# A small store ahead of all others on the store ring, and final waits in the order of the stores, in a group softmax that streams 570 MB

## Chip, cores, metric

One core of one Trainium2 chip, the other cores idle. The time is device microseconds of one execution; lower is better.

## The reference

```python
def reference(x):                       # x: (4, 4096, 4352) float32
    B, N, D = x.shape
    G = 8
    x_g = x.reshape(B, N, G, D // G)
    x_g = x_g - x_g.max(axis=-1, keepdims=True)
    exp = np.exp(x_g)
    out = exp / exp.sum(axis=-1, keepdims=True)
    return out.reshape(B, N, D).astype(np.float32)
```

Softmax over groups of 544 values. The input is read once and the output written once: 285.2 MB each way.

## The kernel before

64 tiles of 256 rows; a tile is 128 partitions x 34816 bytes (4.46 MB), in one of six buffers. SyncE issues all loads (one DMA ring), ScalarE all stores (the other ring). VectorE takes the maxima and scales; ScalarE does the exponentials and their sums. Semaphores tie them together.

```python
    def take(engine, sem, n=1):
        engine.sem_inc(sem, -n).wait_op(sem, n, "sem-ge")
    # ... (vector_max, vector_scale, scalar_exp: one row of each tile half at a time)

    def store(b, target):
        take(nc.scalar, scaled, R)
        nc.scalar.dma_start(out=target, in_=bufs[b][:, :]).then_inc(stored[b], 16)

    def scalar_tile(j, *targets):
        take(nc.scalar, seen)
        for r in range(R):
            if r < len(targets):
                store((j - LAG + r) % NT, targets[r])
            scalar_exp(j * R + r)

    for t in range(nt):                                   # SyncE: loads
        b = t % NT
        if t >= NT:
            nc.sync.wait_ge(stored[b], 16 * (t // NT))
        nc.sync.dma_start(out=bufs[b][:, :], in_=xt[t]).then_inc(landed[b], 16)
    for b in range(NT):                                   # SyncE: the final waits
        nc.sync.wait_ge(stored[b], 16 * ((nt - b + NT - 1) // NT))

    nc.scalar.preload_act_table(Exp)                      # ScalarE
    for j in range(LAG):                                  # LAG = 2
        scalar_tile(j)
    with loop(nc.scalar) as u:
        for b in range(NT):
            scalar_tile(LAG + b, turn_out[u, b])          # first store: in here
    # ... (two last tiles, last stores; VectorE's program)
```

Of the kernel before, what the change touches and what calls it, by code (L numbers as in the profile page):

```python
# [1 line left out]

# [5 lines left out]


@with_exitstack  # L10
def kernel(
    ctx: ExitStack,
    tc: tile.TileContext,
    x: bass.AP,
    out: bass.AP,
):
    nc = tc.nc
    G = 8
    P = 128
    R = 2  # L20
    NT = 6
    S = R * NT
    LAG = 2
    xf = x.flatten_outer_dims()
    of = out.flatten_outer_dims()
    N, D = xf.shape
    Dg = D // G
    nt = N // (P * R)
    turns = (nt - LAG) // NT
    rest = LAG + turns * NT  # L30
    assert rest == nt - 2
    f32 = mybir.dt.float32
    X = mybir.AxisListType.X
    Exp = mybir.ActivationFunctionType.Exp
    xt = xf.rearrange("(t p r) d -> t p (r d)", p=P, r=R)
    ot = of.rearrange("(t p r) d -> t p (r d)", p=P, r=R)
    turn_out = of[:turns * S * P, :].rearrange("(u b p r) d -> u b p (r d)", b=NT, p=P, r=R)

    landed = [tc.alloc_semaphore(f"landed{b}") for b in range(NT)]
    stored = [tc.alloc_semaphore(f"stored{b}") for b in range(NT)]  # L40
    seen = tc.alloc_semaphore("seen")
    max_done = tc.alloc_semaphore("max_done")
    exp_done = tc.alloc_semaphore("exp_done")
    rec_done = tc.alloc_semaphore("rec_done")
    scaled = tc.alloc_semaphore("scaled")

    ctx.enter_context(tc.tile_critical(no_gpsimd_drain=True))  # L47
    bufs = [ctx.enter_context(nc.sbuf_tensor(f"xt{b}", [P, R * D], f32)) for b in range(NT)]
    mx = ctx.enter_context(nc.sbuf_tensor("mx", [P, S, G], f32))
    sm = ctx.enter_context(nc.sbuf_tensor("sm", [P, S, G], f32))  # L50
    rs = ctx.enter_context(nc.sbuf_tensor("rs", [P, S, G], f32))

    def loop(engine):

        return nc.Fori(
            0, turns, engines=OrderedEngineSet([engine.engine]), head_slot={engine.engine: 0})

    def take(engine, sem, n=1):
        engine.sem_inc(sem, -n).wait_op(sem, n, "sem-ge")  # L59

    def row(s):
        b, r = divmod(s, R)
        return bufs[b][:, r * D:(r + 1) * D].rearrange("p (g d) -> p g d", g=G)

    def vector_max(n):
        s = n % S
        if s % R == 0:
            take(nc.vector, landed[s // R], 16)
            nc.vector.sem_inc(seen, 1)
        nc.vector.reduce_max(out=mx[:, s, :], in_=row(s), axis=X, negate=True).then_inc(max_done, 1)  # L70

    def vector_scale(n):
        s = n % S
        take(nc.vector, exp_done)
        nc.vector.reciprocal(out=rs[:, s, :], in_=sm[:, s, :]).then_inc(rec_done, 1)  # L75
        take(nc.vector, rec_done)
        xr = row(s)
        for g in range(G):
            i = nc.vector.tensor_scalar_mul(  # L79
                out=xr[:, g, :], in0=xr[:, g, :], scalar1=rs[:, s, g:g + 1])  # L80
        i.then_inc(scaled, 1)

    def scalar_exp(n):
        s = n % S
        take(nc.scalar, max_done)
        xr = row(s)
        for g in range(G):
            i = nc.scalar.activation(  # L88
                out=xr[:, g, :],
                in_=xr[:, g, :],  # L90
                func=Exp,
                bias=mx[:, s, g:g + 1],
                scale=1.0,
                accum_out=sm[:, s, g:g + 1],
            )
        i.then_inc(exp_done, 1)
# [14 lines that stand above are left out]
    for t in range(nt):  # L111
        b = t % NT
        if t >= NT:
            nc.sync.wait_ge(stored[b], 16 * (t // NT))
        nc.sync.dma_start(out=bufs[b][:, :], in_=xt[t]).then_inc(landed[b], 16)
    for b in range(NT):
        nc.sync.wait_ge(stored[b], 16 * ((nt - b + NT - 1) // NT))


    nc.scalar.preload_act_table(Exp)  # L120
    for j in range(LAG):
        scalar_tile(j)
    with loop(nc.scalar) as u:
        for b in range(NT):
            scalar_tile(LAG + b, turn_out[u, b])
    scalar_tile(nt - 2, ot[nt - 4])
    scalar_tile(nt - 1, ot[nt - 3], ot[nt - 2])
    store((nt - 1) % NT, ot[nt - 1])


    def vector_rows(lo, hi):
        for n in range(lo, hi):
            vector_max(n + 1)
            vector_scale(n)

    vector_max(0)
    vector_rows(0, LAG * R)
    with loop(nc.vector):
        vector_rows(LAG * R, LAG * R + S)
    vector_rows(rest * R, nt * R - 1)  # L140
    vector_scale(nt * R - 1)


# [1 line left out]
_INS = ['x']  # L145
_OUTS = [((4, 4096, 4352), 'float32')]


# [23 lines left out]
```

## Time and profile before

| | before |
|---|---|
| time, median of 3 | 1330.06 us (1329.78 to 1330.08) |
| VectorE, ScalarE busy | 78%, 58% of the span |
| 16 DMA engines busy | 90% or more in 39 of 40 slices |
| first store's issue on ScalarE | 5.47 us; all others 0.34 to 0.35 |
| last store's landing on the 16 engines: middle, last | 1320.41, 1326.77 us |

Read the table from the bottom of the machine upwards: the DMA engines are full, so what changes the time is either bytes, or time in which an engine moves none, or the lag of the last engine. The lines themselves are in the prediction.

I use one derived quantity. **Lost time** at moment T is T minus the time that the bytes finished by then would have taken: T - (bytes finished by T) / (16 x 34816) x 1.2888 us. 1.2888 us is an eighth of the 10.31 us between landings of consecutive loads while only loads run, 8 packets per engine each. The bytes come from the trace's packet records, a packet in flight counted by its elapsed share. In the kernel before it is 2.81 us at 45 us (the start: the first packets begin at 1.96 us and last about 2.1 us) and 3.72 us at 66 us: 0.91 us is lost when the first store begins. After that it stays level or falls slowly.

### The profile page before, as it was taken

The page shows a single profiled execution, that of the slowest core. Times are in us where ns is not written, and L with a number is a line of the kernel's source. Part 1 is how long each engine was busy: PE and PEld are TensorE (multiplying, and loading weights), DVE is VectorE, ACT ScalarE, POOL GpSimd, SP SyncE. Part 2 cuts the span into 40 slices and gives each one's busy share as a digit, 9 for nine tenths or more (in the row PEclk, how much of TensorE's full clock was granted, in tenths as well). Part 3 has the DMA queues.
Part 4 walks back from the last instruction along what each step waited for, and adds up shares of the span by engine and source line. Part 5 has one row for each costly group of instructions (what it writes and reads, how often), then busy time and mean ns, then how long its engine had stood idle before and what let it go on. Part 6 is the DMA issues. An engine that isn't in the chain of part 4 may idle for free. (4 is left out here: it accounts for less than half of the span.)

```text
span 1328.5 us, 4328 instructions
## 1 busy us (share of the span) xinstructions
DVE 1041.7 (78%) x1280; ACT 764.5 (58%) x2049; POOL 0.2 (0%) x4
## 2 busy tenths in 40 slices
DVE  5899987887877878778787787877878778787781
ACT  3677755655556556565565655655556555565551
POOL 0000000000000000000000000000000000000000
DMA  9999999999999999999999999999999999999997
GB/s 403 418 436 435 434 433 429 432 435 436 435 433 428 432 435 436 435 434 430 429 436 435 435 434 433 426 436 436 434 434 433 427 435 436 435 434 433 427 433 328
DMA packets 18439, 570.49 MB, mean 429 GB/s; under 512 B 2048, under 2 KB 2048, under 8 KB 2048
## 3 DMA queue, kind: packets, MB, share of 16 engines
q1 hardware_dynamic: 9216, 285.22, 49.8%
q10 hardware_dynamic: 9216, 285.22, 49.7%
q14 instruction: 7, 0.06, 0.0%
HBM read 285.21 MB, written 285.21 MB: 429 GB/s over the span
## 5 line engine op out<-in xcount | busy, mean ns | idle before, releaser
L88 ACT ACTIVATE xt<-xt,mx 128x544 f32<-128x544 f32 x1024 | 751.3, 735 | 534.1 <-ACTq L59 534.1
L70 DVE TENSOR_REDUCE mx<-xt 128x8 f32<-128x4352 f32 x128 | 599.2, 4682 | 238.3 <-DVEq L59 235.3
L79 DVE TENSOR_SCALAR xt<-xt,rs 128x544 f32<-128x544 f32 x1024 | 434.2, 498 | 19.2
L88 ACT ACTIVATION_READ_ACCUMULATOR xt<-xt,mx 128x1 f32 x1024 | 192.0, 187 | 0.0
L75 DVE RECIPROCAL rs<-sm 128x8 f32<-128x8 f32 x128 | 24.8, 193 | 4.2 <-DVEq L59 4.2
L120 ACT ACT_TABLE_LOAD x1 | 1.3, 1283 | 0.9 <-SPq L47 0.9
L156 POOL MEMSET const-bfloat16-1.0<- 128x1 bf16 x1 | 0.1, 103 | 0.0
L156 POOL MEMSET const-uint8-127<- 128x1 uint8 x1 | 0.1, 102 | 0.0
L156 POOL MEMSET const-float32-0.0<- 128x1 f32 x1 | 0.1, 100 | 0.2 <-issue 0.2
L156 POOL MEMSET const-float32-1.0<- 128x1 f32 x1 | 0.1, 99 | 0.0
## 6 DMA issues: line engine op xcount, KB each, us to landing
xt<-in_x_dram SPq DMA_DIRECT2D x64, 4352.0 KB, 30.5
out_dram<-xt ACTq DMA_DIRECT2D x64, 4352.0 KB, 51.3
```

The source lines that it names most:

```text
L70: nc.vector.reduce_max(out=mx[:, s, :], in_=row(s), axis=X, negate=True).then_inc(max_done, 1)
L75: nc.vector.reciprocal(out=rs[:, s, :], in_=sm[:, s, :]).then_inc(rec_done, 1)
L79: i = nc.vector.tensor_scalar_mul(out=xr[:, g, :], in0=xr[:, g, :], scalar1=rs[:, s, g:g + 1])
L88: i = nc.scalar.activation(out=xr[:, g, :], in_=xr[:, g, :], func=Exp, bias=mx[:, s, g:g + 1], scale=1.0, accum_out=sm[:, s, g:g + 1],)
L120: nc.scalar.preload_act_table(Exp)
L156: nc = _bacc.Bacc("TRN2", target_bir_lowering=False, num_devices=1)
```

## The change

The intent, as the diff tells it: use the store ring once before it matters, so that its first real store finds it ready, and let no satisfied wait follow the last landing. The small store writes 16 x 64 bytes into the output, which tile 0's store overwrites; ScalarE waits for it before the loop, so the two writes are ordered.

```diff
+    first = tc.alloc_semaphore("first")
+    zero = ctx.enter_context(nc.sbuf_tensor("zero", [16, 16], f32))
 ...
-    for b in range(NT):
-        nc.sync.wait_ge(stored[b], 16 * ((nt - b + NT - 1) // NT))
+    for t in range(nt - NT, nt):
+        nc.sync.wait_ge(stored[t % NT], 16 * (t // NT + 1))
 ...
+    take(nc.scalar, first)
+    nc.scalar.dma_start(out=of[0:16, 0:16], in_=zero[:, :]).then_inc(first, 16)
     nc.scalar.preload_act_table(Exp)
     for j in range(LAG):
         scalar_tile(j)
+    take(nc.scalar, first, 16)
     with loop(nc.scalar) as u:
 ...
+    nc.vector.memset(zero[:, :], 0.0).then_inc(first, 1)
     vector_max(0)
```

## The prediction

> **What bounds the kernel now.** I read the page first, for which engine is full and for how long.
>
> ```profile
> DVE 1041.7 (78%) x1280; ACT 764.5 (58%) x2049; POOL 0.2 (0%) x4
> ...
> DMA  9999999999999999999999999999999999999997
> ...
> q1 hardware_dynamic: 9216, 285.22, 49.8%
> q10 hardware_dynamic: 9216, 285.22, 49.7%
> ```
>
> VectorE has 22% of the span to spare and ScalarE 42%; the 16 DMA engines are at 90% or more in 39 of 40 slices. The two rings (q1: loads issued by SyncE, q10: stores issued by ScalarE) take 49.8 + 49.7 = 99.5% of 16 engines' span. So this is a copy of 570 MB with arithmetic beside it. The page's chain of waits ends with the last VectorE work at 1303.5 us and does not see the 23 us of transfers after it, so I leave it and read the waits of the DMA queue and the stretches.
>
> ```profile
> SPq L115 <- DMA out_dram<-xt: 1225.8, 58, 73.6
> SPq L117 <- DMA out_dram<-xt: 77.2, 1, 77.2
> ```
>
> 58 loads wait 1225.8 us in total for a store to free their buffer, and the end of the kernel is a wait for stores. Now busy time and rate by stretch (columns: stretch, length, busy of three engines, clock, DMA share, GB/s):
>
> ```profile
> 20.00:44.00 24.00, 21.91 (x28) 18.96 (x53) 0.00 (x0) 1.00 0.99 427
> 56.00:58.00 2.00, 1.62 (x1) 2.00 (x7) 0.00 (x0) 1.00 1.01 296
> 60.00:80.00 20.00, 19.55 (x28) 14.42 (x41) 0.00 (x0) 1.00 1.03 444
> 80.00:1280.00 1200.00, 961.53 (x1183) 707.35 (x1898) 0.00 (x0) 1.00 1.00 433
> 1318.00:1321.00 3.00, 0.00 (x0) 0.00 (x0) 0.00 (x0) 1.00 0.51 221
> 1321.00:1323.00 2.00, 0.00 (x0) 0.00 (x0) 0.00 (x0) 1.00 0.16 70
> 1323.00:1327.00 4.00, 0.00 (x0) 0.00 (x0) 0.00 (x0) 1.00 0.04 17
> ```
>
> The rate is 433 GB/s for 1200 us. There are two flaws: one at 56 to 58 us, when stores begin, and one after 1320 us, when the share falls to 0.16 and 0.04, about 3 engines and then about one. I looked into both in the trace's packet records (start, duration, queue of each of the 16384 packets of 34816 bytes) and in the landings of the semaphores. Typical packet: 1.288 us on both rings (10th to 90th percentile alike). 1024 packets per engine x 1.288 = 1318.9 us. The last store lands in 16 parts: 13 near 1320.4 us, two at 1322.8, one at 1326.8. That last engine sets the end. It falls behind evenly, from 0.2 us at 91 us to 6.2 us at 1263 us; store packets over 1290 ns add up to about 0.45 us per 100 us, the same rate as its lag of some 0.5 us per 100 us, so I take it that one engine's 512 store packets are each about 12 ns long (6.1 us). I could not attribute packets to engines with certainty; this is an inference.
>
> The first flaw shows in the timeline of ScalarE, here with the last store for comparison:
>
> ```profile
> 48.61 5.47 ACTq L100 DMA_DIRECT2D out_dram<-xt  x1
> 54.21 0.75 ACT L88 ACTIVATE xt<-xt,mx 128x544 f32<-128x544 f32 x1 [6.69 <-ACTq L59]
> ...
> 1303.55 0.34 ACTq L100 DMA_DIRECT2D out_dram<-xt  x1
> ```
>
> The first issue on the store ring holds ScalarE for 5.47 us, any other for 0.34, and its first data packets begin near 58.9 us, 10.3 us after the issue began. Just before, from 56.8 to 57.5 us, each of the 16 engines has a packet of 1.78 to 2.13 us, 0.5 to 0.8 us too long, and six had one 0.14 to 0.42 us too long at 55.5.
>
> **What the Trainium skill says.** (1) "DMA: Bandwidth & Descriptors", section "Issuing engines are not separate DMA queues": issues from several engines run on the same 16 DMA engines and save only sequencer time. The trace agrees: loads alone 433 GB/s from packet times at 20 to 44 us (427 by packet starts above), both rings together 433. (2) Same page, "Queues, rings and completion order": each pair of queue row and engine is its own ring, served in turn. The trace agrees in part: from 58.9 us packets of q1 and q10 alternate. Hence a store whose slowest dimension is 16 would touch the ring once on each engine; the section on the semaphore's increment of 16 says 16 rows go to 16 engines. The trace before has no such store. (3) "Perfetto Trace Analysis", "DMA Instruction — HWDGE": the profiled issue is descriptor generation, and the data movement lies outside. The trace agrees: 0.34 us of issue against 51.3 us median to landing. No page I found says that the first use of a ring costs more.
>
> **The change part by part.**
> Added at the start: a memset of 16x16 on VectorE, estimated at 0.1 us from the GpSimd memsets of 0.10 us; VectorE has nothing until 13.93 us. A wait on ScalarE (0.017 us plus latency), then the small store. If the 5.47 us is the price of the ring's first use, it is now paid from about 1 to 6.5 us. Then comes the table load (1.28 us), done by about 8 us, or a few more if its fetch queues behind loads. ScalarE's first activation starts at 18.74 us, so at least 10 us of slack cover this. Cost on the path: 0. Bytes: 16 x 64 = 1 KB of 570 MB; 16 small packets and 16 completion writes, one of each per engine, well under 0.1 us of an engine's time.
> Added before the loop: one more wait on ScalarE for a store that landed tens of us before, about 0.1 us beside full DMA rings: 0.
> Moved: the first real store should issue in 0.34 us, so ScalarE resumes 5.1 us earlier, and store packets begin perhaps 8 us earlier (near 50 to 51 us). But from 48 to 58 us the engines are not idle: they carry loads 4 and 5. Beginning stores earlier changes which packets go first, not how many there are. Cost or gain on the path: 0.
> Maybe removed: the long packets at 55.5 to 57.5 us, 0.7 us typical per engine and up to 0.9 us on those hit twice. That is true lost engine time, of the slowest engine too, and it shifts the end one for one. At the start it could fall in the first 2 us, where the engines are idle anyway (first packets at 1.96 us, themselves 1.8 to 2.4 us long, so one first-use price is already paid there), or in the middle of the loads, where it costs the same as now. I give 45% to hidden: 0.45 x 0.8 = 0.36 us.
> Moved at the end: the last store to land is tile 63's, in buffer 3. Before, two satisfied waits (buffers 4, 5) follow it; the trace has these waits at 1326.79, 1326.85 and 1326.93 us, so 0.07 us each. In the new order none follows: 2 x 0.07 = 0.14 us gained.
> Sum: 0.36 + 0.14 = 0.5 us: 1330.06 - 0.5 = 1329.5.
>
> **The rivals.**
> Stall only moved. For: a ring's first use under load looks the same wherever it falls. Against: at the start the engines are idle or in their own first packet. Time: 1330.06 - 0.14 = 1329.9.
> The whole delay comes back: 5.1 us of ScalarE, or 8 us of later stores. For: the issue of 5.47 us is the largest single oddity in ScalarE's queue. Against: the DMA engines have no idle stretch between 2 and 1320 us, and the last store is issued at 1303.55 while earlier stores keep the engines full to 1310, so the tail is not short of work either. Time: 1330.06 - 5.1 - 0.14 = 1324.8. I give it 3%.
> The start suffers: ScalarE's slow issue shares descriptor generation with SyncE's six load issues (0.95 to 3.86 us), or delays the table load past 18.7 us. For: both now overlap. Against: SyncE's first load is issued at 0.95 us, before ScalarE can have seen the memset, and one load keeps the engines busy for 10.3 us. A delay of the first packets counts in full; I take 0.5 to 1 us: 1330.5 to 1331. I give it 7%.
> The slow engine changes its lag: with stores starting 8 us earlier the order of packets differs, but 512 store packets remain. Its 6.4 us would change only if the slowness depends on what runs beside it. Time: unchanged but for some tenths.
>
> **Range and chances.** The three runs before span 0.3 us. Between stall moved and stall hidden lie 1329.9 and 1329.1; half a microsecond of run-to-run noise on each side, and a little for a worse start, gives 1328.5 to 1330.5. Two per cent is 26.6 us, more than all flaws found put together (6.4 us tail, under 1 us stall, 2 us start): within 2% 0.98, faster 0.01, slower 0.01.
>
> **What would show each step.** First issue on ScalarE's queue of the small store near 1 us with some 5 us, and then 0.34 us at about 48.6 us: ring's first use confirmed; if it is still 5 us at 48.6, the cost belongs to something else at the loop's entry (code fetched there, for instance). GB/s of 56 to 58 us back at 430 or so: stall gone there; then look from 2 to 12 us for 16 packets of 2 us, besides the first ones: moved. If none: hidden, and the middle landing of the last store comes 0.7 us sooner. Last waits of SyncE: one after the last landing instead of three. The lag of the last engine still 6 to 6.5 us. The prediction is wrong if the engines turn out to have idle time that earlier stores fill, if the slow engine's lag moves by more than 1 us, or if the start of the first load slips.

## The result, and the profile after

| | before | after |
|---|---|---|
| median of 4 runs | 1330.07 us (1329.78 to 1330.17) | 1329.86 us (1329.41 to 1330.28) |
| ratio | | 0.9999, 95% interval 0.9981 to 1.0016: same |

(Ratios are the mean time of one kernel's runs over that of the other's of the same rounds, so not quite the ratio of these medians.) The ratio cannot tell 0.2 us from nothing; what follows about tenths of microseconds is read from the two traces.

ScalarE's own stores and the small one in the changed kernel (durations in ns: shortest/median/longest, then first and last start in us):

```profile
L102 ACTq DMA_DIRECT2D out_dram<-xt x64: 337/339/376, 48.2 to 1302.3; - x64
L124 ACTq DMA_DIRECT2D out_dram<-zero x1: 398/398/398, 1.2 to 1.2; - x1
```

The long issue is gone from the first real store, 0.376 us at 48.2 us, and it is not found at the start either: the small store takes 0.398 us. Nothing was moved; 5.1 us of ScalarE's queue vanished. The start itself, in order of time (start, length):

```profile
0.95 3.09 SPq L117 DMA_DIRECT2D xt<-in_x_dram  x6
1.00 0.07 DVE L142 MEMSET zero<- 16x16 f32 x1 [1.00 <-SPq L48]
1.18 0.40 ACTq L124 DMA_DIRECT2D out_dram<-zero  x1
1.61 1.28 ACT L125 ACT_TABLE_LOAD   x1 [1.61 <-ACTq L61]
```

The table load is as long as before (1.28 us). The first load's last part lands at 13.91 us instead of 13.70.

ScalarE at its first real store, to be compared with the 5.47 us in the prediction:

```profile
48.25 0.38 ACTq L102 DMA_DIRECT2D out_dram<-xt  x1
50.01 0.75 ACT L90 ACTIVATE xt<-xt,mx 128x544 f32<-128x544 f32 x1 [2.28 <-ACTq L61]
```

ScalarE resumes at 50.01 us, 4.20 us earlier than before (54.21). Yet the second store is issued at 63.95 us, where it was issued at 63.08 before. The first row ends early, and then ScalarE waits for VectorE, whose next maximum starts at 57.26 us, where it started at 56.38 before. VectorE passed the branch into its loop at 50.49 us (before: 50.27), and its maximum starts 1.5 us after an 8192-byte packet on the instruction queue has ended (55.44 + 0.31 = 55.75 us); before, 1.6 us after one ended at 54.74. So VectorE seems to wait for the code of its loop, 6 to 7 us after the branch, and the packet came later in the changed kernel. ScalarE shows the same at its own loop: it passes the branch at 43.50 us (before: 43.21) and issues the first real store at 48.25 us (48.61), 1.7 us after an instruction packet has ended (46.59 and 46.88). In all 13 kernels that have this branch the first store in the loop comes 1.66 to 1.73 us after such a packet; in peel below, which has no branch there, it is issued at 43.45 us. The lead was given back within 10 us of being won; it could not have shortened the span anyway, with the engines full.

The same stretches as in the prediction, after the change (stretch, length, busy of VectorE, ScalarE, GpSimd, clock, DMA share, GB/s):

```profile
20.00:44.00 24.00, 21.91 (x28) 18.97 (x53) 0.00 (x0) 1.00 0.99 429
44.00:54.00 10.00, 9.39 (x14) 7.72 (x22) 0.00 (x0) 1.00 0.98 380
56.00:58.00 2.00, 0.74 (x1) 0.00 (x0) 0.00 (x0) 1.00 1.09 470
80.00:1280.00 1200.00, 962.72 (x1187) 708.11 (x1902) 0.00 (x0) 1.00 1.00 433
1318.00:1321.00 3.00, 0.00 (x0) 0.00 (x0) 0.00 (x0) 1.00 0.54 232
1321.00:1323.00 2.00, 0.00 (x0) 0.00 (x0) 0.00 (x0) 1.00 0.12 52
1323.00:1327.00 4.00, 0.00 (x0) 0.00 (x0) 0.00 (x0) 1.00 0.04 17
```

The stretch 44 to 54 us of the kernel before, which the prediction doesn't show:

```profile
44.00:54.00 10.00, 9.18 (x13) 3.52 (x10) 0.00 (x0) 1.00 0.98 423
```

56 to 58 us is clean now, but 44 to 54 us fell from 423 to 380 GB/s: the flaw went with the first real store. (A rate here counts a packet's bytes where the packet starts.) Packets of 1.3 to 2.6 us start between 49.0 and 51.4 us. They are packets of loads; the first store packets follow at 52.5 us and take the usual 1.29 us. It is the same in the kernel before: long load packets start up to 57.5 us, store packets from 58.0 us. Lost time grows from 2.80 us (at 45 us) to 3.94 (at 66 us): 1.14 us, against 0.91 before. The tail is as it was, about two engines and then one: middle landing of the last store 1320.60 us, last 1326.86 us, a lag of 6.27 us against 6.37.

The final waits (waiter, waited for, us, times, longest):

```profile
SPq L119 <- DMA out_dram<-xt: 75.8, 3, 55.3
```

Before it was 77.2 us once: all hung on one semaphore, and the rest was then satisfied. Now three waits are real, and the last is the last landing. SyncE's first step after the waits starts 0.22 us after its wait on the last landing (1326.88 to 1327.10 us), before 0.36 us (1326.79 to 1327.15): 0.14 us.

### The profile page after: what moved, and what is told of

Read it like the earlier page. It is cut to its first block, busy times and chain, and to the rows that moved or that the text cites. A ratio compares the mean times of both kernels' runs of the same rounds, so it can differ in the third digit from the quotient of the medians.

```text
span 1328.4 us, 4332 instructions
## 1 busy us (share of the span) xinstructions
DVE 1041.5 (78%) x1281; ACT 764.4 (58%) x2049; POOL 0.2 (0%) x4
```

## The experiments

All give correct results. The times of runs with one execution say little below 1 us. The table gathers what was measured; "early" is lost time between 15 and 25 us, "at store" between 45 and 66 us.

| kernel | time, us | first issue on the ring: at, us, and length | first real store: at and issue | early | at store |
|---|---|---|---|---|---|
| before | 1330.07 | 48.61, 5.466 | the same | -0.03 | 0.91 |
| after | 1329.86 | 1.18, 0.398 | 48.25, 0.376 | -0.03 | 1.14 |
| rows128 | 1330.39 | 1.19, 0.386 | 47.20, 0.361 | -0.03 | 1.05 |
| rows128_2k | 1331.06 | 1.71, 0.421 | 47.81, 0.360 | -0.02 | 1.00 |
| warm_late | 1329.23 | 26.45, 0.398 | 47.24, 0.382 | -0.03 | 0.86 |
| peel | 1329.77 | 43.45, 4.737 | the same | -0.03 | 1.09 |
| late128 | 1330.32 | 26.29, 0.386 | 47.33, 0.360 | -0.03 | 0.98 |
| early_full16 | 1333.37 | 14.06, 0.398 | 53.38, 0.376 | 2.72 | 0.09 |
| early_full128 | 1342.84 | 14.26, 0.386 | 69.95, 0.360 | 0.96 | none by 66 us |
| early_8k | 1330.56 | 14.06, 0.399 | 50.03, 0.376 | 0.02 | 0.94 |
| pad3 | 1330.83 | 47.02, 5.485 | the same | -0.03 | 1.05 |
| after_pad125 | 1329.50 | 1.18, 0.398 | 49.75, 0.372 | -0.02 | 1.03 |
| tail120 | 1339.35 | 1.19, 0.392 | 47.13, 0.382 | -0.03 | 1.04 |
| order_only | 1329.89 | 48.41, 5.475 | the same | -0.03 | 0.87 |

Two questions: what the lost microsecond is, and what the long issue is. My first theory, from the prediction, was one answer for both: the first use of the ring. The after trace had already parted them, since the one stayed and the other went.

### rows128 and rows128_2k: does the loss come with the first touch of the rows?

```diff
-    zero = ... [16, 16]
+    zero = ... [P, 16]            # rows128_2k: [P, 512]
-    nc.scalar.dma_start(out=of[0:16, 0:16], in_=zero[:, :]).then_inc(first, 16)
+    nc.scalar.dma_start(out=ot[0][:, 0:16], in_=zero[:, :]).then_inc(first, 16)   # _2k: 0:512
```

> The small store goes out first as in the changed kernel, but as 128 rows of 64 bytes, one in each row that tile 0's store writes later, so 8 data packets per DMA engine instead of 1. Theory (bulk): the lost engine time at the first real store comes with the first 34816-byte packets of the store ring, so it stays: about 0.9 to 1.2 us per engine between 48 and 56 us, as in the changed kernel (1.05). Rival (first touch): it comes with the first write to each of these rows or with filling 9 descriptors of the ring, so it moves to the first 10 us and the loss at 48 to 56 us falls under 0.3 us. Both: issue near 1.2 us takes about 0.4 us, time 1329 to 1331 us.

> As the run with 128 rows, with 2048 bytes in each row (262 KB, an estimated 0.6 us of the 16 engines at 433 GB/s; memset of 128x512 an estimated 0.5 us before it). Theory (bulk, any size): if some 2 KB in each packet are enough to count as bulk, the loss moves to the start; if not, it stays near 1 us at 48 to 56 us. Rival (first touch): under 0.3 us left there. Time: 0.3 to 0.8 us longer than the changed kernel for the added bytes, so 1330.2 to 1331.

The loss stayed at the first real store, 1.05 and 1.00 us. So neither the first write to each of the 128 rows of tile 0 nor eight data packets per engine on the ring take it away, and packets of 2048 bytes don't count either. The second kernel was timed in rounds: 1331.06 us median (1329.59 to 1331.47) beside 1330.79 for the kernel before, ratio 0.9998, interval 0.9981 to 1.0014: same; the predicted 0.3 to 0.8 us for its bytes cannot be seen in the times. (In this chip's rounds the kernel before had three of 8 runs at 1331.89, 1332.58 and 1339.88 us.)

### warm_late: the small store under load

```diff
-    take(nc.scalar, first)
-    nc.scalar.dma_start(out=of[0:16, 0:16], in_=zero[:, :]).then_inc(first, 16)
     for j in range(LAG):
         scalar_tile(j)
+        if j == 0:
+            take(nc.scalar, first)
+            nc.scalar.dma_start(out=of[0:16, 0:16], in_=zero[:, :]).then_inc(first, 16)
```

> The small store of 16 rows of 64 bytes is issued after the first tile's exponentials (near 30 us), when loads keep all 16 DMA engines full, not at the start. Theory (first use of the ring under load costs the issuing queue): this issue takes about 5 us and the first real store 0.3 to 0.4 us. Rival (the 5.47 us of before belongs to the loop's entry or to a big store): this issue takes 0.3 to 0.5 us, and then the first real store too, since the ring has been used. The loss of engine time at the first real store stays 0.8 to 1.2 us in the theory; if a ring's first use under load were its cause, it would move to 30 to 38 us. Time 1329 to 1331 us.

```profile
L102 ACTq DMA_DIRECT2D out_dram<-xt x64: 338/339/382, 47.2 to 1301.4; - x64
L128 ACTq DMA_DIRECT2D out_dram<-zero x1: 398/398/398, 26.4 to 26.4; - x1
```

Here my theory fell: the first use of the ring, at 26.4 us with every engine loading, took 0.398 us. And the rival fell as well in its plain form, since the first real store in the loop was then quick at 47.2 us. The loss did not move to this store: 0.86 us at the real one. The time of 1329.23 us is the lowest, but it is one execution; its last landing is 0.87 us earlier than before's, with a lag of 5.55 us on the last engine, which nothing in this kernel explains.

### peel: no loop entry before the first store

```diff
-    with loop(nc.scalar) as u:
+    for b in range(NT):
+        scalar_tile(LAG + b, ot[b])
+    with loop(nc.scalar, 1) as u:      # ScalarE's loop starts at turn 1; kernel before otherwise
```

> The kernel before, with ScalarE's first turn of the loop written out ahead of it, so that the first six stores have fixed addresses and no loop entry stands before the first one. Theory (first use of the ring under load): the first store's issue still takes 4 to 6 us, and the loss of engine time near 57 us stays 0.7 to 1.1 us. Rival (loop entry, its code fetch or register addresses): the issue takes 0.3 to 0.5 us and the loss near 57 us is gone. Time 1329 to 1331 us.

```profile
43.45 4.74 ACTq L100 DMA_DIRECT2D out_dram<-xt  x1
43.80 0.19 ACT L88 ACTIVATION_READ_ACCUMULATOR xt<-xt,mx 128x1 f32 x1
43.90 0.73 ACT L88 ACTIVATE xt<-xt,mx 128x544 f32<-128x544 f32 x1
```

Neither the loop entry nor register addresses make it: the issue is at 43.45 us, in straight code with fixed addresses, and takes 4.74 us. ScalarE's exponentials go on meanwhile (the lines below it), so here the long issue is hidden. The loss is 1.09 us, between 48 and 52 us.

### late128, early_full16, early_full128: descriptors, size, or the first full store

```diff
 # late128: warm_late with 128 rows
-            nc.scalar.dma_start(out=of[0:16, 0:16], in_=zero[:, :]).then_inc(first, 16)
+            nc.scalar.dma_start(out=ot[0][:, 0:16], in_=zero[:, :]).then_inc(first, 16)
 # early_full16 (early_full128: 0:128): changed kernel without zero; in scalar_tile, after take(seen)
+        if j == 0:
+            nc.scalar.dma_start(out=ot[0][0:16, :], in_=bufs[0][0:16, :]).then_inc(first, 16)
+            take(nc.scalar, first, 16)
```

> The small store goes out near 26 us, with all engines loading, as 128 rows of 64 bytes: as many descriptors per engine (8, and one for the semaphore) as a full store. In the run with 16 rows at that place the issue took only 0.40 us, so 'first use under load costs 5 us' fell. Theory (count): the first store on the ring holds the queue when it has many descriptors and the engines are full, because the descriptors wait for the ring to be served: issue 4 to 6 us here. Rival (size): the long issue needs 34816-byte rows: issue 0.3 to 0.5 us here. The first real store then takes under 0.5 us in both. Loss of engine time at the first real store 0.7 to 1.1 us in both. Time 1329 to 1331 us.

> In place of the small store, 16 whole rows of 34816 bytes of tile 0 as it was loaded go out near 14 us (1 data packet per engine; overwritten by tile 0's store; ScalarE waits for them). Theory (first large packet): the loss of 0.8 to 1.1 us of engine time moves to 15 to 24 us and less than 0.3 us is lost at the first real store. Rival (sustained mixing of loads and stores, or the first full store): the loss stays at the first real store near 50 us. The added bytes cost 1.3 us of every engine in both: 1330.5 to 1332 us.

> As the run with 16 whole rows, with all 128 rows of tile 0 (8 data packets per engine, 4.46 MB). Theory (first full store): the loss of 0.8 to 1.1 us moves to this store, and less than 0.3 us is lost when the real stores begin; the issue near 14 us takes about 5 us, since the engines are loading and the ring is unused. Rival (something in the program at 48 to 57 us): the loss stays there and the early issue takes 0.4 us. The added bytes cost 10.3 us of every engine: 1339 to 1342 us.

The stretches 15 to 25 us and 45 to 66 us of early_full16, and then of early_full128, which is followed by its early issue:

```profile
15.00:25.00 10.00, 8.32 (x2) 0.00 (x0) 0.00 (x0) 1.00 1.00 313
45.00:66.00 21.00, 16.98 (x21) 12.51 (x34) 0.00 (x0) 1.00 1.00 431
```

```profile
15.00:25.00 10.00, 8.52 (x2) 0.00 (x0) 0.00 (x0) 1.00 0.98 383
45.00:66.00 21.00, 18.26 (x26) 15.97 (x43) 0.00 (x0) 1.00 0.99 429
```

```profile
14.26 0.39 ACTq L107 DMA_DIRECT2D out_dram<-xt  x1
```

The low rate stands in the first stretch and not in the second: in the kernel before it is the other way round (446 and 423 GB/s by the same view). With whole rows the loss goes where the first of them go. One packet per engine is enough: early_full16 lost 0.09 us when its real stores began. But nothing is gained. Its 16 packets took 3.5 to 4.6 us each, and 2.72 us were lost there; with the packet itself (1.29 us) less the 0.82 us not lost later (0.91 - 0.09) that makes 3.2 us, and the last landing is at 1330.03 us, 3.26 us after before's. early_full128 lost 0.96 us there, and in another form: its early store packets all took 1.29 us, and load packets of 1.4 to 3.1 us stand just ahead of them, as at the first real store of the kernel before. So the 2.72 us of early_full16 may in part belong to its split, 16 rows with one for each engine; no run separates this. early_full128 also lost 2.22 us between 70 and 100 us: 0.8 us from 86 to 88 us, when loads had drained, the second real store was issued only at 86.16 us, and few of the engines had a packet; then 1.3 us with long packets (up to 2.4 us) from 92 us, when loads come back. Its longer time is then 8 x 1.2888 = 10.3 us for the bytes and 2.2 us for that, 12.5; the last landing came 12.7 us later. I had not expected the second part. Why loads coming back cost time here, and not at 80 us in the kernel before, stays open; it also means that such a loss need not come only once.

For the long issue: late128 (0.386 us) clears the number of descriptors, and early_full128 (0.386 us at 14.26 us, a full store, never used ring, every engine loading) clears size and load together. My expectation of 4 to 6 us in late128 and of about 5 us in early_full128 was wrong.

### early_8k: the size of the packet

```diff
-            nc.scalar.dma_start(out=ot[0][0:16, :], in_=bufs[0][0:16, :]).then_inc(first, 16)
+            nc.scalar.dma_start(out=ot[0][0:16, 0:2048], in_=bufs[0][0:16, 0:2048]).then_inc(first, 16)
```

> The run with 16 whole rows at 14 us, cut to the first 8192 bytes of each row. There, 34816-byte rows moved the loss of engine time to 18 to 24 us and left under 0.1 us at the first real store; 64 and 2048 bytes left it at the real store. Theory (packets over some size between 2 and 34 KB): either the loss is here (over 0.5 us lost between 15 and 25 us beyond the bytes, under 0.3 us near 55 us), or it stays at the real store at 0.7 to 1.1 us; the run tells which side of 8192 bytes the size lies. Time 1330 to 1332.5 us.

Lost time early 0.02 us, at the real store 0.94 us. This kernel differs from early_full16 in the bytes of a row alone, so the size decides: somewhere between 8192 and 34816 bytes the ring's first packets start to cost the engines time. Its 16 packets took 0.31 to 0.38 us each. With one packet for each engine, the size of a packet and the bytes of an engine are the same thing here; which of the two counts is not tested.

### pad3 and after_pad125: does ScalarE wait for its own code?

The long issue ended shortly after an 8192-byte packet on the instruction queue in both kernels that had it by then, and all kernels with a short one have two or three instructions more ahead of the store.

```diff
 # pad3: kernel before, 3 increments; after_pad125: changed kernel, 125, after the small store
+    for _ in range(3):
+        nc.scalar.sem_inc(pads, 1)
     nc.scalar.preload_act_table(Exp)
```

> The kernel before with three do-nothing semaphore increments at the start of ScalarE's program and no small store: ScalarE's instructions lie three places later, as in the changed kernel. Theory (the 5.47 us is ScalarE waiting for its own code: the long issues of the kernel before and of the peeled one end 1.38 and 1.34 us after an 8192-byte packet on the instruction queue ended, the short ones all came with two or three instructions ahead of them): the first store's issue falls to 0.3 to 0.5 us though the ring was never used. Rival (only an earlier store on the ring helps): 4.5 to 6 us. Loss of engine time at the first store 0.7 to 1.1 us in both. Time 1329 to 1331 us.

> The changed kernel, small store and all, with 125 do-nothing increments on ScalarE after the small store (some 70 ns each, 9 us in all, done before ScalarE has work at 18.7 us): with the three instructions of the change ScalarE's code lies 128 places later[...]. Theory (code fetch): the place in a fetched block is that of the kernel before again, so the first full store's issue is long again, 4 to 6 us, in spite of the small store. Rival (small store makes the ring ready): 0.3 to 0.5 us. If an instruction isn't 64 bytes, a short issue leaves this open. Time 1329 to 1331 us.

The first store's line of pad3, then of after_pad125:

```profile
L101 ACTq DMA_DIRECT2D out_dram<-xt x64: 338/338/5485, 47.0 to 1304.1; - x64
```

```profile
L103 ACTq DMA_DIRECT2D out_dram<-xt x64: 338/339/372, 49.8 to 1301.7; - x64
```

Both against the theory: three places of shift do not shorten the issue, and a shift that I took for a whole block does not lengthen it (this second run counts only if 128 instructions do fill a block, which no run measured). So it is an earlier DMA on ScalarE's queue that helps, not the place of the code. What parts the two groups of kernels is when the queue's first issue comes: by 27 us in all the short ones, after 43 us in all the long ones. What is left of the code fetch is a coincidence in time that is too regular to drop: all four long issues end 1.34 to 1.38 us after an instruction packet has ended (before: packet 52.39 + 0.31 = 52.70, issue ends 54.08; peel: 46.85 and 48.19; pad3: 51.13 and 52.51; order_only: 52.51 and 53.89). In the traces with a short first issue, at 1.2 to 1.7, 14 and 26 us, no instruction packet runs near that issue: from 1 to 43 us there is only one, at 9.09 us in after_pad125.

### order_only: the waits alone

```diff
-    for b in range(NT):
-        nc.sync.wait_ge(stored[b], 16 * ((nt - b + NT - 1) // NT))
+    for t in range(nt - NT, nt):
+        nc.sync.wait_ge(stored[t % NT], 16 * (t // NT + 1))
```

> The kernel before with the final waits in the order of the stores and nothing else. All theories: from the last landing to the end of the waits one wait instead of three, 0.14 us less between the last landing and the end of the span (1.6 instead of 1.7 us); the first store's issue 5 us as before, the loss at the first store 0.7 to 1.1 us. If the issue is short here, chance decides it and not the program. Time 1329.5 to 1330.5 us.

```profile
SPq L117 <- DMA out_dram<-xt: 77.1, 3, 56.6
```

Three real waits instead of one; SyncE's next step starts 0.22 us after the wait on the last landing (1326.57 to 1326.79), as in the changed kernel, so the 0.14 us is the reordering alone. The first issue is 5.475 us: the reordering has nothing to do with it.

### tail120: a try at the last engine

```diff
-    store((nt - 1) % NT, ot[nt - 1])
+    b = (nt - 1) % NT
+    take(nc.scalar, scaled, R)
+    nc.scalar.dma_start(out=ot[nt - 1][0:120, :], in_=bufs[b][0:120, :]).then_inc(stored[b], 16)
+    nc.scalar.dma_start(out=ot[nt - 1][120:128, :], in_=bufs[b][120:128, :]).then_inc(tailed, 16)
```

> The changed kernel with its last store cut into 120 partitions (15 engines, 8 rows each) and 8 partitions (8 engines, one row each), so that one engine has no packet of it and eight have 9. If the engine that ends 6.3 us late is the one left out, it ends 10.3 us sooner and the end is set by the engines 2 to 3 us late, with one more packet at most: 1323 to 1324.3 in the trace instead of 1326.9, time 1326.5 to 1328. If it is one of the eight, it has one packet more: 1331 us. If it is neither: 1330 us. Issue of the two stores about 0.7 us instead of 0.34, hidden behind the queued stores.

```profile
1280.00:1308.00 28.00, 18.76 (x29) 11.93 (x32) 0.00 (x0) 1.00 1.01 438
1308.00:1320.00 12.00, 0.00 (x0) 0.00 (x0) 0.00 (x0) 1.00 1.01 305
1320.00:1330.00 10.00, 0.00 (x0) 0.00 (x0) 0.00 (x0) 1.00 0.52 146
```

None of the three cases I foresaw came: 1339.35 us median (1339.30 to 1339.70) against 1330.12, ratio 1.0069, interval 1.0055 to 1.0082, clearly 9 us longer. The rate falls to 305 GB/s with the DMA share still 1.01, so the engines are not idle; packets last up to 5.2 us instead of 1.288. With this split the packets are slow; whether the uneven number does it, or which rows an engine gets, no run separates (the 16 rows of early_full16, one for each engine, were slow too, at 3.5 to 4.6 us). Which engine lags stays unknown.

## Why the prediction was right

The time was right (1329.5 predicted, 1329.86 measured, range 1328.5 to 1330.5) for its main reason, and two terms of its sum were wrong by a few tenths. That the number came out within 0.4 us is in part luck: without the wrong term of 0.36 us it is 1329.9, the number of the rival "stall only moved", and the times can't tell the two apart, since the four runs after span 0.9 us. That rival's mechanism failed as well: the stall did not move to the small store. Two small readings were off: 1330.06 - 0.5 is 1329.56, and the trace has 15 long packets, not 16, between 56.8 and 57.5 us.

- **The engines are full, so no shift of ScalarE's work reaches the end.** Right, and shown by the traces: 4.2 us earlier on ScalarE, about 5 us earlier for store packets (first ones at 52.5 to 54.4 us, before 58.0 to 59.3), and the middle landing of the last store moved by +0.19 us. The prediction had said packets from 50 to 51 us. early_full16 and early_full128 show the other side: bytes and lost time reach the end nearly in full (3.2 of 3.26 us, 12.5 of 12.7).
- **The 5.47 us as the price of the ring's first use, now paid from 1 to 6.5 us.** This step failed. The first use cost 0.40 us at the start, at 14 us and at 26 us, with the engines full or not. An earlier store does remove the long issue; why it is long only when the ring's first store comes at 43 us or later is not settled. A reading that fits all the traces, only argued: the ring's first issue waits if a block of code for ScalarE is being fetched at that moment. The test would be the small store issued as the ring's first in that very moment; no run here did it.
- **The long packets perhaps hidden at the start: 0.45 x 0.8 = 0.36 us.** This term is 0 at best. The loss went with the first real store and was 1.14 us instead of 0.91. The runs replace "first use of the ring" by "first packets over some size between 8192 and 34816 bytes": stores with rows of 64, 2048 and 8192 bytes left the loss at the real store, both with whole rows took it away from there. Why such packets cost time is not shown. Over the twelve kernels whose first whole-row packets are their real stores, this loss is 0.86 to 1.14 us, so the difference of 0.23 us between before and after is within what varies.
- **Two satisfied waits fewer: 0.14 us.** Right, 0.36 to 0.22 us, and order_only has it alone.
- **The start does not suffer.** Right: the first load's last part is 0.2 us later, and lost time at 45 us is 2.80 against 2.81.
- **The last engine's lag stays at 6 to 6.5 us.** Right: 6.27. That one engine's store packets are each 12 ns long remains an inference; the lag was there in all 13 kernels whose last store is whole (5.5 to 6.5 us).

The sum as it came out: +0.09 us at the last landing (+0.19 at the middle one, -0.10 of lag), -0.14 for the waits, in all about -0.05 us in the trace, and 0.2 us in the medians, which is noise.

## What to carry to other kernels

When the DMA engines are full from end to end, ask of every oddity on an issuing engine's queue whether it leaves an engine without bytes; 5 us on ScalarE were worth nothing here, and 1 us on the engines at most 1 us. Count the bytes finished against time: such a curve shows in one number where engine time is lost, and it told a moved loss from a removed one when the busy share said 0.9 or more nearly everywhere. A warm-up must resemble what it warms for; test it at the place and size in question before believing in it.

## What the Trainium skill lacked or had wrong

- "DMA: Bandwidth & Descriptors", "Specifications": it gives some 27 GiB/s per engine. Here a packet of 34816 bytes takes 1.288 us on one engine in loads and in stores, 27.0 GB/s, so 25.2 GiB/s; 16 engines give 433 GB/s, near the 435 GB/s of the same table. The unit is what differs.
- No page says that the engines lose time when the first packets of 34816 bytes of a store ring come: 0.86 to 1.14 us per engine here at the first real store, and nothing of the kind with 64, 2048 or 8192 bytes.
- "Perfetto Trace Analysis", "DMA Instruction — HWDGE": the profiled issue is a wait for the lock, descriptor generation and the last semaphore push. Nothing there lets one expect a first issue of 4.7 to 5.5 us where others of the same form take 0.34; an earlier store on the queue, of any size tried, removed it.
- "DMA: Bandwidth & Descriptors", "Latency and other measured facts": as its best guess it puts slower engines down to software-generated descriptors. All DMAs here come from SyncE and ScalarE, and still the last of the 16 landings comes 5.5 to 6.5 us after the middle one in all 13 kernels whose last store is whole.
- The same page, "Why a DMA increments its semaphore by 16 and not by 1": the rule for the number of engines agrees with tail120 (one count at once and 15 later for 120 partitions, 8 for 8). It does not say that packets can be slow with such a split: up to 5.2 us instead of 1.288, and 305 GB/s instead of 438.
- "Runtime: NRT & Kernel Launch", "Instruction fetch mechanics": it has the stall for code after a taken branch, but not its length under full DMA engines. Here VectorE's first maximum in its loop starts 5.8 to 8.2 us after its branch (13 traces; one lacks the branch) and 1.5 to 1.6 us after an 8192-byte packet of the instruction queue (all 14); ScalarE's first store in its loop comes 3.4 to 6.1 us after its branch (13).
